# One decoder layer with 32 experts: all expert pairs in written order, side work split over four places

## The chip, the cores and the metric

The kernel runs on one core of one Trainium2 chip. The metric is the device time of one execution in microseconds. Three runs of the kernel before took 611.28, 612.3 and 613.26 us; the median, 612.3, is what the prediction is measured against. One further execution was profiled.

## The reference, cut to what matters

All data are float32; 256 tokens of 1024 features, one layer.

```python
h = x
a = rms_norm(h, g_mix);  z = a @ w_in                  # pool channels | q | k | v | forget logits
h = h + concat(causal_pool_mixer(...), forgetting_attention(...)) @ w_out
# hierarchical mixture of experts: 4 groups of 8 experts, each 1024 -> 512 -> 1024
t = rms_norm(h, g_ffn)
grp = argmax(t @ w_grp + b_grp)                        # one group per token
top2 of the 8 experts of that group, weights comb      # two experts per token
for g in range(4):
    hg = einsum('nd,edf->nef', t, w_e_gate[g]);  hu = einsum('nd,edf->nef', t, w_e_up[g])
    y += einsum('nef,efd->nd', silu(hg) * hu * comb[:, g, :, None], w_e_down[g])
h = h + y
gate = sigmoid(rms_norm(h, g_ple) @ w_ple_gate)        # 1024 x 1024
h = h + gate * (p @ w_ple_proj)
out = rms_norm(h, g_final)
```

The weights of the 32 experts are 201 MB of the 221 MB that are read.

## The kernel before, in words

The first part (mixer, attention, output projection, routing) is not touched by the change. Then come the experts in 16 **pairs** of two, `pi` 0 to 15. Each expert has 32 slots for tokens; four experts (two pairs) make a **quad** `q`, eight experts (four pairs) a **group** `g` of up to 128 tokens.

For a pair, `gate_up(pi, kh)` (L927) multiplies the slots' rows by the gate and up weights, half of the 1024 inputs at a time (`kh`). Two experts times gate and up are four 32-column tiles, written to four quarters of one accumulator, so that four matmuls with different column tiles stand side by side on TensorE. A float32 matmul counts as two in the profile. `hidden` (L938) is SiLU on ScalarE and a product on VectorE; `hidden_transposes` (L944) four transposes and a copy; `down` (L953) the down weights, again with four column tiles; `stack` (L965) copies the result to `ys`, one half on ScalarE, one on VectorE.

Beside the pairs stands work by group and quad, with full-width matmuls:
- `compact(g)` (L869) collects a group's rows `Xc` with matmuls; `one_hots`, `gather(q, kh)` (L902) and `scatter_weights(q)` (L913) make a quad's inputs `xgs` and the matrix `sws`; `scatter(q)` (L972) adds the experts' results by token in accumulators `Y`.
- When a group's two quads are done: `add_rows` (L1062) adds `Y` to the rows on VectorE, `half_norm` (L1068) makes the norm (squares on ScalarE, eight small steps on VectorE), `turn` (L1082) transposes the rows, `z_direct(g, ms)` (L1091) multiplies them by the gate matrix in eight steps `m` (the accumulators `Z`), `embedding_rows` (L1102) picks the group's rows of the embedding, and `finish` (L1113) applies the gate, the last norm and writes the rows with an indirect DMA of GpSimd.

`group_ends` and `group_body` (L1283 to L1313) put this work in lists `todo[pi][0..2]`, which `fill` calls at three places of a pair: after the first half of gate-up, after `hidden`, and after `stack`. The last group can't wait for its last quad: before pair 15, `last_slots`, `turn`, and `z_direct` of group 3 run on the rows as they are, and what the quad's results add to Z is added later (`z_rows` for pair 14, `z_rows1` for pair 15, whose two experts 30 and 31 are worked one after the other).

What sets the order: up to L1042 and from L1358 on, TensorE, VectorE and ScalarE run in the order in which the code is written (`manual_schedule`). Between, for pairs 2 to 14, a planner decides, by its own costs and due times, in which order each engine runs what the code asks for; the calls of `fill` only set priorities there. At pair 8 stands a conditional block (`dense_path`, not taken with these inputs).

The weights come in pieces of 1 MiB through SyncE's queue into buffers of that size that are used in turn (`stream`, L789); a piece is issued when the matmuls that read the buffer's last content are done. Twelve pieces make a pair: gate and up of both experts for the first input half, the same for the second, then down. PSUM has two buffers for accumulators of a pair (`acc`), two for transposes and gathers (`tb_`) and four for `Y` and `Z`.

Of the kernel before, what the change touches and what calls it, by code (L numbers as in the profile page):

```python
# [13 lines left out]
AF = mybir.ActivationFunctionType  # L14
# [10 lines left out]
def layer_kernel(ctx, tc, x, p, g_mix, w_in, b_f, w_pool, s_pool, w_out, g_ffn, w_grp, b_grp,  # L25
                 w_rt, b_rt, w_e_gate, w_e_up, w_e_down, g_ple, w_ple_gate, w_ple_proj, g_final, out):
    nc = tc.nc
# [3 lines left out]
    NP, NQ = NE // 2, NE // 4  # L31
# [8 lines left out]
    def acc(name):  # L40
        return psA.tile([128, 512], F32, tag="acc", name=name)

    def tb_(name):
        return psA.tile([128, 512], F32, tag="t", name=name)
# [113 lines left out]
    def sumsq(dst, src, name):  # L158

        junk = wk.tile([128, src.shape[1]], BF, tag="b", bufs=2, name=name)  # L160
        return nc.scalar.activation(junk, src, AF.Square, scale=D ** -0.5, accum_out=dst)
# [84 lines left out]
    for g, w in enumerate(WINDOWS):  # L246
# [2 lines left out]


    in_order = ExitStack()
    in_order.enter_context(tc.manual_schedule(engines={mybir.EngineType.PE, mybir.EngineType.DVE,
                                                       mybir.EngineType.Activation}))
    aTh = region(0, "aTh", F32R).rearrange("p (k t) -> p k t", k=8)
    aTl = region(1, "aTl", F32R).rearrange("p (k t) -> p k t", k=8)

# [600 lines left out]
    def small(g):  # L857
        if g not in smalls:
            smalls[g] = st.tile([128, 8], F32, name=f"small{g}")
        return smalls[g]  # L860

    def in_group(g):

        pg_ = wk.tile([128, 2, 128], F32, tag="c0", name=f"ing{g}")
        for tb in range(2):
            nc.vector.tensor_scalar(pg_[:, tb, :], place1, place[:, tb, g:g + 1], None, op0=ALU.is_equal)
        return pg_
# [76 lines left out]
    def hidden_transposes(pi, act):  # L944
        pa = tb_(f"pa{pi}")
        for c in range(4):
            nc.tensor.transpose(pa[:, c * 64:(c + 1) * 64], act[64:128, c * 128:(c + 1) * 128],  # L947
                                ident[64:128, 64:128])
        at = wk.tile([128, 4, 64], F32, tag="b", bufs=2, name=f"at{pi}")
        nc.vector.tensor_copy(at, pa[:, :256].rearrange("p (c s) -> p c s", c=4))  # L950
        return at

    def down(pi, act, dn):  # L953

        at = hidden_transposes(pi, act)
        pd = acc(f"pd{pi}")
        for c in range(4):
            for gI in range(4):
                j, dh = gI % 2, gI // 2
                nc.tensor.matmul(pd[32 * gI:32 * gI + 32, :], lhsT=at[:, c, 32 * j:32 * j + 32],  # L960
                                 rhs=dn[j, c // 2](c % 2)[:, dh * 512:(dh + 1) * 512],
                                 start=c == 0, stop=c == 3, tile_position=(0, 32 * gI))
        return pd
# [75 lines left out]
    for kh in range(2):  # L1039
        gather(1, kh, orr)  # L1040
    scatter_weights(1, oq)
    in_order.close()  # L1042


    gpm = gp.rearrange("p q k -> p (q k)")
    hTs, PPc, Z, ss3, r3 = {}, {}, {}, {}, {}
    LG = 3

    def chunk2(m):
# [12 lines left out]
    def add_rows(g):  # L1062

        for dh in range(2):
            xs = Xc[g][:, dh * 512:(dh + 1) * 512]
            nc.vector.tensor_add(xs, xs, Ys[g][dh])

    def half_norm(g):  # L1068

        s = small(g)[:, 1:3]  # L1070
        for dh in range(2):
            sumsq(s[:, dh:dh + 1], Xc[g][:, dh * 512:(dh + 1) * 512], f"sq3{g}{dh}")
        r3[g] = small(g)[:, 3:4]
        rsqrt(r3[g], s[:, 0:1], s[:, 1:2], f"r3s{g}", 0.5)

# [23 lines left out]
                nc.tensor.matmul(Z[g][i][:, 0:c], lhsT=hTs[g][:, m, :], rhs=wpg[m // 2](m % 2)[:, c * i:c * i + c],  # L1099
                                 start=m == 0, stop=m == 7 and g != LG)  # L1100

    def embedding_rows(g):  # L1102

        pg_ = in_group(g)
        PPc[g] = fins[g][:, 1024:2048]
        for dh in range(2):
            ds = slice(dh * 512, (dh + 1) * 512)
            pp = tb_(f"ppc{g}{dh}")
            for tb in range(2):
                nc.tensor.matmul(pp, lhsT=pg_[:, tb, :], rhs=PP[:, tb, ds], start=tb == 0, stop=tb == 1)  # L1110
            nc.scalar.activation(PPc[g][:, ds], pp, AF.Copy, scale=0.5)

    def finish(g, sg, o):  # L1113

# [100 lines left out]
        nc.gpsimd.dma_start(out[0].rearrange("(b p) d -> p b d", p=128), X)  # L1215


    def rows_of_quad(q, khs=range(2)):
        if 0 in khs:
            oqs[q] = one_hots(q)  # L1220
        for kh in khs:
            gather(q, kh, oqs[q][1])
        if 1 in khs:
            scatter_weights(q, oqs[q][0])

    oqs = {}
    yTs, zls, ysl, zsl = {}, {}, {}, {}
# [49 lines left out]
    def new_fin(g):  # L1277
        fins[g] = fin_tile(g)

    def scatter_q(q):  # L1280
        scatter(q, yss[q])

    def group_ends(g):  # L1283

        p, e = 4 * g, g - 1
        todo[p][0] += [lambda: scatter_q(2 * g - 1), lambda: add_rows(e), lambda: half_norm(e)]
        todo[p][1] += [lambda: rows_of_quad(2 * g + 1, (0,))]
        todo[p][2] += [lambda: rows_of_quad(2 * g + 1, (1,)), lambda: new_fin(e), lambda: turn(e, 0),
                       lambda: turn(e, 1)]
        ends = [lambda: embedding_rows(e), lambda: finish(e, fins[e][:, 0:1024], fins[e][:, 1024:2048])]  # L1290
        if g == LG:
            todo[p][2] += [lambda: z_direct(e, range(0, 3))]
            todo[p + 1][0] += [lambda: z_direct(e, range(3, 6))]
            todo[p + 1][1] += [lambda: z_direct(e, range(6, 8)), ends[0]]
            todo[p + 1][2] += [ends[1]]
        else:
            todo[p + 1][0] += [lambda: z_direct(e, range(0, 3))]
            todo[p + 1][1] += [lambda: z_direct(e, range(3, 5))]
            todo[p + 1][2] += [lambda: z_direct(e, range(5, 7))]
            todo[p + 2][0] += [lambda: z_direct(e, range(7, 8))]  # L1300
            todo[p + 2][1] += [ends[0]]
            todo[p + 2][2] += [ends[1]]

    todo = {pi: [[], [], []] for pi in range(2, NP - 1)}

    def group_body(g):
        todo[4 * g + 2][0].append(lambda: scatter_q(2 * g))
        todo[4 * g + 2][1].append(lambda: row_numbers(g))
        if g < LG:
            todo[4 * g + 3][0].append(lambda: compact(g + 1))  # L1310
            todo[4 * g + 3][1].append(lambda: rows_of_quad(2 * g + 2, (0,)))
            todo[4 * g + 3][2].append(lambda: rows_of_quad(2 * g + 2, (1,)))

    for g in range(4):
        group_body(g)
        if g:
            group_ends(g)
    todo[2][2].append(lambda: embedding(*emb))
    todo[4][1].append(last_gain)
    todo[12][0] += [lambda: new_fin(LG), lambda: embedding_rows(LG)]  # L1320
    todo[14][0] += [lambda: add_rows(LG)]
    todo[14][1] += [last_slots, lambda: turn(LG, 0), lambda: turn(LG, 1), lambda: z_direct(LG, range(0, 2))]
    todo[14][2] += [lambda: gained(14), lambda: z_direct(LG, range(2, 8))]
    rv = nc.values_load(ovi[0:1, 0:1], min_val=0, max_val=1)

    def fill(pi, n):
        for f in todo[pi][n]:
            f()

    for pi in range(2, NP - 1):  # L1330
        gu, dn = pair_w
        if pi == 2:
            PP = region(whole_region(), "PP").rearrange("p (b d) -> p b d", b=2)
            emb = load_embedding()
        if pi == 4:
            wpg = load_gate()
            r_ht = whole_region()
            gfB = quarter(3, "gfB")
        if pi == 8:
            fill(pi, 0)  # L1340
            with tc.If(rv > 0):  # L1341
                dense_path()
        pair_w = load_pair(pi + 1)
        pg = acc(f"pg{pi}")
        gate_up(pi, 0, gu, pg)
        if pi != 8:
            fill(pi, 0)
        if pi % 2 == 0:
            yss[pi // 2] = quarter(1, f"ys{pi // 2}")
        gate_up(pi, 1, gu, pg)  # L1350
        act = hidden(pi, pg)
        fill(pi, 1)
        pd = down(pi, act, dn)
        stack(pi, pd, yss[pi // 2])
        fill(pi, 2)


    ctx.enter_context(tc.manual_schedule(engines={mybir.EngineType.PE, mybir.EngineType.DVE,  # L1358
                                                  mybir.EngineType.Activation}))
    pi, Q = NP - 1, NQ - 1  # L1360
    gu, dn = pair_w
    ys, Zl = yss[Q], Z[LG]
# [87 lines left out]
                                 rhs=wpg[m // 2](m % 2)[:, 256 * g:256 * g + 256],  # L1450
                                 start=m == 0, stop=m == 7, tile_position=(0, 32 * g))

    z_rows(pi - 1, range(2))
    gate_up1(0, 0)
    z_rows(pi - 1, range(2, 6))
    gate_up1(0, 1)
    hidden1(0)
    z_rows(pi - 1, range(6, 8))
    hidden_transposes1(0)
    for dh in range(2):  # L1460
        down1(0, dh, lambda c: dn[0, c // 2](c % 2)[:, 512 * dh:512 * dh + 512])
    for dh in range(2):
        gained1(0, dh)
        for g in range(4):
            nc.gpsimd.tensor_copy(ys[rows_of(0), chunk2(4 * dh + g)], wide[32 * g:32 * g + 32, 0, dh, :])
# [25 lines left out]
    ys1 = y_last(1)  # L1491
    z_rows1(1, range(4, 8))
    add_last(1, ys1)
    half_norm(LG)
    pair_of((zh, zlo), zl1[1][:, 0:256])

    for g in range(4):
        rs = slice(32 * g, 32 * g + 32)
        for n, part in enumerate((zh, zlo)):
            nc.tensor.matmul(Zl[g][:, 0:256], lhsT=sw1[rs, :], rhs=part[rs, :], start=False, stop=n == 1,  # L1500
                             tile_position=(32 * g, 0))
    finish(LG, fins[LG][:, 0:1024], last_o)


# [26 lines left out]
```

## Time and profile before

| what | value |
|---|---|
| median of three runs | 612.3 us (611.28 to 613.26) |
| the profiled execution | 611.7 us, its span 610.1 us |
| TensorE matmul busy | 534.2 us (88%) |
| VectorE, ScalarE, GpSimd busy | 176.4, 117.9, 40.7 us |
| moved by DMA | 222.54 MB, 365 GB/s over the span |
| TensorE's granted clock, mean | 0.937 |

The span runs from the first to the last instruction; the execution takes 1.6 us more. "Busy" of TensorE is from the start of matmuls to their modelled ends, so matmuls on several column tiles count once. A clock of 1.0 is 2.4 GHz, 0.5 is 1.2 GHz; a stretch's value is the mean over it. The chain of waits goes back from the last instruction, at each step to what released it or to the instruction before it on its engine.

### The profile page before, as it was taken

The numbers are of one execution on the slowest core, as the hardware profiler recorded it, in microseconds if no ns is written. First come the engines' busy times: TensorE is split into PE (matmuls) and PEld (weight loads), VectorE is DVE, ScalarE is ACT, GpSimd is POOL, SyncE is SP. The second block draws the span as 40 slices with busy tenths as digits, with TensorE's granted clock in tenths as the row PEclk, the third lists the DMA queues.
The fourth block names the chain that finished last, engine by engine and source line by source line (L and its number), as shares of the span: only waits on it lengthen the run. The fifth ranks groups of instructions, "written<-read, shape, count | busy, mean of one in ns | idle before, by whom it ended". The sixth has DMA issues, their size and how long they took to land. (4 is left out here: it accounts for less than half of the span.)

```text
span 610.1 us, 7828 instructions
## 1 busy us (share of the span) xinstructions
PE 534.2 (88%) x3139; PEld 253.8 (42%) x3139; DVE 176.4 (29%) x461; ACT 117.9 (19%) x246; POOL 40.7 (7%) x82
## 2 busy tenths in 40 slices
PE   7999999978899999987976799989797998997890
PEld 6899778533333434221312233223141332452450
DVE  5677665233111221030303110223022103301234
ACT  4553564111011110110201000111011002000142
POOL 6095000000000000000000000000000000000100
PEclk9999999699989889997879789999799899999996
DMA  8989957599999999999999999999999999999400
GB/s 293 342 291 417 404 203 274 232 414 415 408 418 415 416 417 421 413 420 413 421 414 419 411 417 413 414 414 416 414 413 415 414 414 416 413 371 367 172 2 17
DMA packets 55734, 222.54 MB, mean 365 GB/s; under 512 B 8714, under 2 KB 15630, under 8 KB 42254
## 3 DMA queue, kind: packets, MB, share of 16 engines
q1 hardware_dynamic: 55086, 220.94, 90.9%
q0 software_dynamic: 608, 1.05, 0.5%
q8 instruction: 26, 0.43, 0.3%
q14 instruction: 14, 0.11, 0.1%
HBM read 220.93 MB, written 2.10 MB: 366 GB/s over the span
## 5 line engine op out<-in xcount | busy, mean ns | idle before, releaser
L934 PE MATMUL pg<-wu,xg 128*32 128x512 f32 x480 | 131.0, 641 | 11.6 <-DMA wu<-in_w_e_up_dram 11.6
L934 PE MATMUL pg<-wg,xg 128*32 128x512 f32 x472 | 132.8, 639 | 9.3 <-PEq L1341 5.8
L960 PE MATMUL pd<-wd,at 128*32 128x512 f32 x480 | 80.8, 668 | 3.3 <-DVE at L950 1.6
L1099 PE MATMUL Z<-wpg,fin 128*128 128x512 f32 (+1 forms) x160 | 60.9, 521 | 0.9 <-DVE fin L1087 0.9
L941 DVE TENSOR_TENSOR act<-act,pg 64x512 f32<-64x512 f32 x15 | 10.4, 692 | 174.4 <-ACT act L940 174.4
L934 PEld LDWEIGHTS pg<-wu,xg 128*32 128x32 f32 x480 | 29.8, 116 | 65.8 <-issue 39.9
L934 PEld LDWEIGHTS pg<-wg,xg 128*32 128x32 f32 x472 | 28.8, 115 | 56.5 <-issue 44.9
L1099 PEld LDWEIGHTS Z<-wpg,fin 128*128 128x128 f32 x160 | 28.6, 189 | 34.1 <-issue 31.2
L940 ACT ACTIVATE act<-pg 64x512 f32<-64x512 f32 x15 | 8.8, 589 | 167.6 <-PE pg L934 167.6
L908 PEld LDWEIGHTS pgx<-oq,xrows 128*128 128x128 f32 x112 | 28.2, 331 | 15.2 <-issue 10.4
L960 PEld LDWEIGHTS pd<-wd,at 128*32 128x32 f32 x480 | 16.0, 118 | 43.8 <-issue 36.1
L908 PE MATMUL pgx<-oq,xrows 128*128 128x128 f32 x112 | 32.2, 425 | 1.3 <-ACT xrows L883 1.3
L1130 POOL DMA_INDIRECT out_dram<-fin,rowi x3 | 3.0, 1005 | 400.1 <-DVE fin L1129 400.1
L947 PE MATMUL pa<-ident,act 64*128 64x64 f32 x60 | 6.9, 235 | 18.7 <-DVE act L941 18.7
L910 DVE TENSOR_TENSOR xg<-pgx,gf 128x512 f32<-128x512 f32 x14 | 9.7, 692 | 42.6 <-PE pgx L908 42.6
L968 DVE COPY ys<-pd 64x512 f32<-64x512 f32 x15 | 10.4, 694 | 39.7 <-ACT ys L967 39.7
L967 ACT COPY ys<-pd 64x512 f32<-64x512 f32 x15 | 8.7, 578 | 62.5 <-PE pd L960 62.4
L275 PE MATMUL po<-sp_o,cTh 128*128 128x512 f32 x64 | 20.7, 404 | 0.0
L978 PE MATMUL Y<-ys,sw 128*128 128x512 f32 x28 | 15.8, 687 | 3.6 <-ACT ys L967 3.6
L947 PEld LDWEIGHTS pa<-ident,act 64*128 64x128 f32 x60 | 4.8, 138 | 32.2 <-DVE act L941 30.5
L1110 PE MATMUL ppc<-PP,ing 128*128 128x512 f32 x32 | 16.3, 622 | 0.0
L882 PE MATMUL xc<-X,ing 128*128 128x512 f32 x32 | 15.8, 617 | 0.0
(360 smaller groups left out, 678.2 us busy)
## 6 DMA issues: line engine op xcount, KB each, us to landing
wu<-in_w_e_up_dram SPq DMA_DIRECT2D x52, 1024.0 KB, 12.6
wg<-in_w_e_gate_dram SPq DMA_DIRECT2D x49, 1024.0 KB, 13.4
wd<-in_w_e_down_dram SPq DMA_DIRECT2D x49, 1024.0 KB, 19.1
wd<-in_w_e_down_dram SPq DMA_DIRECT2D x30, 512.0 KB, 10.9
wg<-in_w_e_gate_dram SPq DMA_DIRECT2D x28, 512.0 KB
wu<-in_w_e_up_dram SPq DMA_DIRECT2D x24, 512.0 KB, 15.4
w_o<-in_w_out_dram SPq DMA_DIRECT2D x4, 1024.0 KB, 5.8
wpg<-in_w_ple_gate_dram SPq DMA_DIRECT2D x4, 1024.0 KB, 16.3
```

The lines of the kernel that those rows point to most:

```text
L275: nc.tensor.matmul(o, lhsT=a, rhs=b, start=first and i == 0, stop=last and i == 2)
L882: nc.tensor.matmul(px, lhsT=pg_[:, tb, :], rhs=X[:, tb, ds], start=tb == 0, stop=tb == 1)
L908: nc.tensor.matmul(pg[:, k4 * 128:(k4 + 1) * 128], lhsT=Xc[q // 2][:, 4 * kh + k4::8], rhs=orr, start=True, stop=True)
L910: nc.vector.tensor_tensor(xgs[q][:, 4 * kh:4 * kh + 4, :], pg.rearrange("p (k t) -> p k t", k=4), gf[:, 4 * kh:4 * kh + 4, None].to_broadc ...
L934: nc.tensor.matmul(pg[32 * c:32 * c + 32, :], lhsT=xg[:, k, sl:sl + 32], rhs=gu["gu"[c // 2], j, kh](k % 4), start=k == 0, stop=k == 7, ti ...
L941: nc.vector.tensor_mul(act[64:128, :], act[64:128, :], pg[64:128, :])
L947: nc.tensor.transpose(pa[:, c * 64:(c + 1) * 64], act[64:128, c * 128:(c + 1) * 128], ident[64:128, 64:128])
L960: nc.tensor.matmul(pd[32 * gI:32 * gI + 32, :], lhsT=at[:, c, 32 * j:32 * j + 32], rhs=dn[j, c // 2](c % 2)[:, dh * 512:(dh + 1) * 512], s ...
L968: nc.vector.tensor_copy(ys[rs, 512:1024], pd[64:128, :])
L978: nc.tensor.matmul(Ys[g][dh], lhsT=sws[q], rhs=ys[:, dh * 512:(dh + 1) * 512], start=q % 2 == 0, stop=q % 2 == 1 or last)
L1099: nc.tensor.matmul(Z[g][i][:, 0:c], lhsT=hTs[g][:, m, :], rhs=wpg[m // 2](m % 2)[:, c * i:c * i + c], start=m == 0, stop=m == 7 and g != LG)
L1110: nc.tensor.matmul(pp, lhsT=pg_[:, tb, :], rhs=PP[:, tb, ds], start=tb == 0, stop=tb == 1)
```

## The change

Pairs 2 to 14 now run in written order on TensorE, VectorE and ScalarE as well; only the conditional block at pair 8 is left to the planner. The lists have four places: after the first half of gate-up (0), after `hidden` (1), between the transposes' copy and the down matmuls (2, new), and after `stack` (3). The work is dealt out anew: Z in single steps, the two halves of `embedding_rows` separately, `add_rows` and `half_norm` later, and the norm cut into squares and root. Embedding rows of group 3 stand at pair 11 instead of 12; at pair 14 group 3's rows, `last_slots`, `turn` and the first Z step stand in place 0, and Z steps 6 and 7 go into pair 15, where `z_rows` of pair 14 move back behind gate-up and down of expert 30. At the very end the root of the norm stands behind the split of the last Z rows.

```diff
-    in_order.enter_context(tc.manual_schedule(engines={mybir.EngineType.PE, mybir.EngineType.DVE,
-                                                       mybir.EngineType.Activation}))
+    ordered = {mybir.EngineType.PE, mybir.EngineType.DVE, mybir.EngineType.Activation}
+    in_order.enter_context(tc.manual_schedule(engines=ordered))
...
         at = hidden_transposes(pi, act)
+        if between:
+            between()
         pd = acc(f"pd{pi}")
...
     scatter_weights(1, oq)
-    in_order.close()
...
+    def plan(pi, *places):
+        for have, new in zip(todo[pi], places):
+            have.extend(new)
+
+    def zs_of(g, *ms):
+        return [lambda m=m: z_direct(g, (m,)) for m in ms]
+
+    def quad_rows(q):
+
+        return ([lambda: new_quad(q), lambda: gather(q, 0, oqs[q][1])], [lambda: gather(q, 1, oqs[q][1])],
+                [lambda: scatter_weights(q, oqs[q][0])])
+
+    def group_body(g):
+        plan(4 * g + 2, [lambda: scatter_q(2 * g), lambda: row_numbers(g)])
+        if g < LG:
+            plan(4 * g + 3, [lambda: compact(g + 1)], *quad_rows(2 * g + 2))
+
     def group_ends(g):
 
         p, e = 4 * g, g - 1
...
+        rows = quad_rows(2 * g + 1)
+        plan(p, [lambda: scatter_q(2 * g - 1)], rows[0], rows[1] + [lambda: add_rows(e)],
+             rows[2] + [lambda: new_fin(e), lambda: turn(e, 0), lambda: turn(e, 1), lambda: half_norm(e)])
+        emb2 = [lambda dh=dh: embedding_rows(e, dh) for dh in range(2)]
+        end = [lambda: finish(e, fins[e][:, 0:1024], fins[e][:, 1024:2048])]
         if g == LG:
...
+            plan(p, [], [], [], zs_of(e, 0, 1))
+            plan(p + 1, zs_of(e, 2, 3, 4), zs_of(e, 5), zs_of(e, 6), zs_of(e, 7) + emb2 + end)
         else:
...
+            plan(p + 1, zs_of(e, 0, 1, 2), zs_of(e, 3), zs_of(e, 4), zs_of(e, 5, 6, 7))
+            plan(p + 2, [], emb2[:1], emb2[1:], end)
...
+    plan(2, [], [], [], [lambda: embedding(*emb)])
+    plan(4, [], [], [], [last_gain])
+    plan(11, [], [], [], [lambda: new_fin(LG), lambda: embedding_rows(LG, 0), lambda: embedding_rows(LG, 1),
+                          lambda: row_numbers(LG)])
+    plan(14, [lambda: add_rows(LG), last_slots, lambda: turn(LG, 0), lambda: turn(LG, 1)] + zs_of(LG, 0),
+         zs_of(LG, 1, 2), zs_of(LG, 3), zs_of(LG, 4, 5) + [lambda: gained(14)])
...
-        pd = down(pi, act, dn)
+        pd = down(pi, act, dn, lambda: fill(pi, 2))
         stack(pi, pd, yss[pi // 2])
-        fill(pi, 2)
-
-
-    ctx.enter_context(tc.manual_schedule(engines={mybir.EngineType.PE, mybir.EngineType.DVE,
-                                                  mybir.EngineType.Activation}))
+        fill(pi, 3)
...
-    z_rows(pi - 1, range(2))
     gate_up1(0, 0)
-    z_rows(pi - 1, range(2, 6))
+    z_direct(LG, (6, 7))
     gate_up1(0, 1)
     hidden1(0)
-    z_rows(pi - 1, range(6, 8))
+    z_rows(pi - 1, range(2))
     hidden_transposes1(0)
+    z_rows(pi - 1, range(2, 3))
     for dh in range(2):
         down1(0, dh, lambda c: dn[0, c // 2](c % 2)[:, 512 * dh:512 * dh + 512])
+    z_rows(pi - 1, range(3, 8))
...
-    half_norm(LG)
+    half_squares(LG)
     pair_of((zh, zlo), zl1[1][:, 0:256])
+    half_root(LG)
```

## Rows read from the trace of the kernel before

**Rows 1.** Page, 40 slices of 15.25 us: TensorE, its clock, DMA in tenths, GB/s.
```profile
PE   7999999978899999987976799989797998997890
PEclk9999999699989889997879789999799899999996
DMA  8989957599999999999999999999999999999400
GB/s 293 342 291 417 404 203 274 232 414 415 408 418 415 416 417 421 413 420 413 421 414 419 411 417 413 414 414 416 414 413 415 414 414 416 413 371 367 172 2 17
```

**Rows 2.** Windows: stretch, length, busy time (instructions) by engine, TensorE's clock, DMA share, GB/s.
```profile
280.00:345.00 65.00, 51.20 (x241) 16.90 (x245) 12.91 (x39) 7.38 (x16) 1.08 (x1) 0.82 1.02 415
345.00:468.00 123.00, 108.68 (x520) 35.80 (x512) 22.93 (x57) 13.76 (x27) 0.96 (x1) 0.96 1.02 414
530.00:560.00 30.00, 27.35 (x155) 13.76 (x153) 1.20 (x3) 1.17 (x2) 0.00 (x0) 1.00 0.93 366
571.00:610.00 39.00, 23.14 (x364) 13.31 (x356) 16.02 (x46) 13.92 (x37) 3.58 (x9) 0.85 0.03 10
471.74:584.84 113.10, 103.70 (x673) 44.40 (x673) 20.74 (x43) 13.73 (x30) 3.56 (x9) 0.97 0.87 350
```

**Rows 3.** Chain of waits from 468 to 590 us: start, length, engine, tile, line, instructions.
```profile
468.08 3.63 PE pg L934 x26
...
481.61 1.12 PE Z L1099 x2
...
491.11 0.97 PE pg L934 x2
...
494.00 0.97 PE pg L934 x2
494.97 3.63 PE Z L1099 x8
498.60 0.98 PE pg L934 x2
...
501.49 3.56 PE pg L934 x28
...
514.34 0.60 ACT act L940
...
522.07 0.59 ACT ys L967
...
573.89 1.14 issue
...
583.11 1.73 PE pg L1380 x32
```

**Rows 4.** Timeline of SyncE's queue, 522 to 560 us: start, length, the loads issued.
```profile
523.90 3.01 SPq L799 DMA_DIRECT2D wg<-in_w_e_gate_dram  x1
539.37 0.34 SPq L799 DMA_DIRECT2D wu<-in_w_e_up_dram  x1
...
557.96 1.67 SPq L799 DMA_DIRECT2D wd<-in_w_e_down_dram  x2
```

**Rows 5.** Timeline of TensorE where it waits for the last up-weights (pairs 11, 12).
```profile
436.78 1.06 PE L934 MATMUL pg<-wu,xg 128*32 128x512 f32 x1 [0.97 <-DMA wu<-in_w_e_up_dram]
...
468.08 0.62 PE L934 MATMUL pg<-wu,xg 128*32 128x512 f32 x1 [1.48 <-DMA wu<-in_w_e_up_dram]
```

**Rows 6.** Timeline of TensorE at the gather of a quad's first half.
```profile
454.48 1.93 PE L908 MATMUL pgx<-oq,xrows 128*128 128x128 f32 x8
```

**Rows 7.** VectorE groups from 400 us on: line, shapes, count, busy us, mean ns, idle before.
```profile
L1122 DVE SCALAR_TENSOR_TENSOR fin<-fin 128x512 f32<-128x512 f32 x4 | 2.8, 688 | 20.1 <-ACT fin L1111 18.7 <-ACT fin L1120 1.3
...
L896 DVE TENSOR_TENSOR oq<-auxc,slot 128x128 f32<-128x128 f32 x2 | 0.6, 288 | 0.0
```

**Rows 8.** Timeline from 594 to 598 us: first step of the root, split of Z.
```profile
595.02 0.21 DVE L133 TENSOR_SCALAR r3s<-small 128x1 f32<-128x1 f32 x1 [0.80 <-ACT sq L161]
...
596.62 0.41 DVE L1412 TENSOR_TENSOR zhl<-zl,zhl 128x256 fp32r<-128x256 f32 x1
```

More of the change, by code (lines that the diff above doesn't have):

```diff
@@ L951, in hidden_transposes, with down @@
         return at
-    def down(pi, act, dn):
+    def down(pi, act, dn, between=None):
         at = hidden_transposes(pi, act)
+        if between:
+            between()
         pd = acc(f"pd{pi}")
@@ L1041, in layer_kernel @@
     scatter_weights(1, oq)
-    in_order.close()
     gpm = gp.rearrange("p q k -> p (q k)")
-    hTs, PPc, Z, ss3, r3 = {}, {}, {}, {}, {}
+    hTs, PPc, Z, r3, ings = {}, {}, {}, {}, {}
     LG = 3
@@ L1068, in half_norm, with half_squares, half_root @@
     def half_norm(g):
+        half_squares(g)
+        half_root(g)
+    def half_squares(g, dhs=range(2)):
+        for dh in dhs:
+            sumsq(small(g)[:, 1 + dh:2 + dh], Xc[g][:, dh * 512:(dh + 1) * 512], f"sq3{g}{dh}")
+    def half_root(g):
         s = small(g)[:, 1:3]
-        for dh in range(2):
-            sumsq(s[:, dh:dh + 1], Xc[g][:, dh * 512:(dh + 1) * 512], f"sq3{g}{dh}")
         r3[g] = small(g)[:, 3:4]
@@ L1100, in z_direct, with embedding_rows @@
                                  start=m == 0, stop=m == 7 and g != LG)
[L1102 to L1111, printed above, removed]
+    def embedding_rows(g, dh):
+        if dh == 0:
+            ings[g] = in_group(g)
+            PPc[g] = fins[g][:, 1024:2048]
+        ds = slice(dh * 512, (dh + 1) * 512)
+        pp = tb_(f"ppc{g}{dh}")
+        for tb in range(2):
+            nc.tensor.matmul(pp, lhsT=ings[g][:, tb, :], rhs=PP[:, tb, ds], start=tb == 0, stop=tb == 1)
+        nc.scalar.activation(PPc[g][:, ds], pp, AF.Copy, scale=0.5)
     def finish(g, sg, o):
@@ L1215, in dense_path, with new_quad @@
         nc.gpsimd.dma_start(out[0].rearrange("(b p) d -> p b d", p=128), X)
[L1218 to L1224, printed above, removed]
+    def new_quad(q):
+        oqs[q] = one_hots(q)
     oqs = {}
@@ L1281, in scatter_q @@
         scatter(q, yss[q])
+    todo = {pi: [[], [], [], []] for pi in range(2, NP - 1)}
+    def plan(pi, *places):
[10 more added lines that the diff above has]
+            plan(4 * g + 3, [lambda: compact(g + 1)], *quad_rows(2 * g + 2))
@@ L1283, in group_ends @@
     def group_ends(g):
         p, e = 4 * g, g - 1
[L1286 to L1290, printed above, removed]
+        rows = quad_rows(2 * g + 1)
@@ L1291, in group_ends @@
+        plan(p, [lambda: scatter_q(2 * g - 1)], rows[0], rows[1] + [lambda: add_rows(e)],
+             rows[2] + [lambda: new_fin(e), lambda: turn(e, 0), lambda: turn(e, 1), lambda: half_norm(e)])
+        emb2 = [lambda dh=dh: embedding_rows(e, dh) for dh in range(2)]
+        end = [lambda: finish(e, fins[e][:, 0:1024], fins[e][:, 1024:2048])]
         if g == LG:
-            todo[p][2] += [lambda: z_direct(e, range(0, 3))]
-            todo[p + 1][0] += [lambda: z_direct(e, range(3, 6))]
-            todo[p + 1][1] += [lambda: z_direct(e, range(6, 8)), ends[0]]
@@ L1295, in group_ends @@
-            todo[p + 1][2] += [ends[1]]
-        else:
[L1297 to L1312, printed above, removed]
+            plan(p, [], [], [], zs_of(e, 0, 1))
@@ L1317, in layer_kernel @@
             group_ends(g)
[L1318 to L1323, printed above, removed]
+    plan(2, [], [], [], [lambda: embedding(*emb)])
[4 more added lines that the diff above has]
+         zs_of(LG, 1, 2), zs_of(LG, 3), zs_of(LG, 4, 5) + [lambda: gained(14)])
     rv = nc.values_load(ovi[0:1, 0:1], min_val=0, max_val=1)
@@ L1340, in layer_kernel @@
             fill(pi, 0)
+            in_order.close()
             with tc.If(rv > 0):
                 dense_path()
+            in_order.enter_context(tc.manual_schedule(engines=ordered))
         pair_w = load_pair(pi + 1)
@@ L1502, in layer_kernel @@
     finish(LG, fins[LG][:, 0:1024], last_o)
+    in_order.close()
 _INS = ['x', 'p', 'g_mix', 'w_in', 'b_f', 'w_pool', 's_pool', 'w_out', 'g_ffn', 'w_grp', 'b_grp',
```

## The prediction

> **What bounds the kernel now.** I read the slices of the page first [rows 1]. From about 122 us to 530 us the DMA engines are full and move 411 to 421 GB/s, so the weight stream sets the pace there; TensorE is busy 70 to 99% beside it. Then the rate sags (371, 367, 172 GB/s in slices 36 to 38), and after it there is no traffic. The windows give sizes [rows 2]: 414 to 415 GB/s from 280 to 468 us, 366 from 530 to 560, and 39 us after the last weights (571 to 610) in which almost nothing is loaded.
>
> Next the chain of waits from 468 us on [rows 3]. Its first row there is TensorE starting on the last up-weights of pair 12, which landed at 468.08; from that point no link of the chain is a transfer. TensorE is behind the stream: pair 13's gate-up begins in single pieces at 491.11, and the last gate-up piece of pair 15 starts at 583.11 and ends at 584.84. The SyncE timeline says the same from the other side [rows 4]: after a load issued by 526.91 it issues nothing until 539.37, since the buffers are not released, and the last two loads start at 557.96. So: the stream bounds until 468, TensorE from 468 to 585, and a chain through ScalarE and VectorE from 585 to the end. Only the last two can move by an order of work.
>
> **Part 1: work that is no longer cut up.** In the chain, two matmuls of one 32-column tile stand alone between full-width ones: 0.97, 0.97 and 0.98 us at 491.11, 494.00 and 498.60, and the other 28 of that half then take 3.56 us as if all 32 were there [rows 3]. The tile alone takes almost as long as four tiles side by side. Such a lone pair costs 0.95 us; the chain has 11 of them between 475 and 546 us (one in pair 12's down part before the Z work and one after it, three in pair 13's first half, one in its second, three and two in pair 14's halves). In written order each half of gate-up and each down part is one block. 11 x 0.95 = 10.5 us go.
>
> The Trainium skill ("TensorEngine Tiling (Array Packing)", Key Properties) says that a change of tiling mode drains TensorE. By that rule alone the loss would be the drain at each switch; the row nearest to it is a Z group of two at 1.12 us (481.61) against 0.91 for two of a run of eight (494.97, 3.63 us) [rows 3], so 0.1 to 0.2 us, some 2 us in all, and the change would be worth 2 us here. The rows above decide against it: they show a whole pass lost, not a drain.
>
> **Part 2: work between 471.74 (pair 12's SiLU) and 584.84.** TensorE is busy 103.70 of these 113.10 us [rows 2]; 9.4 are waits. Minus the 10.5 above; minus 3.4 for the two stretches of half clock (mean 0.97 over the window: 3% of 113 us, which at half clock is 6.8 us, 1.2 GHz instead of 2.4, of which half is lost); plus 1.93 for the gather of quad 7's first half, which stood at 454.48 [rows 6] and now comes behind pair 12's SiLU. That leaves 91.7 us of work at full clock. The half-clock time I count as gone because its return would mostly lie in the waits on transfers below.
>
> **Part 3: the waits that the written order makes.** Going through the queue in order, with durations from the rows: SiLU 0.60 and ScalarE's copy 0.59 [rows 3], a pass of VectorE over 512 columns 0.69, a one-hot 0.29 [rows 7]:
> - Pair 12: the gather sits behind two one-hots that sit on VectorE behind the product and so behind SiLU, 0.60+0.69+0.58: 1.9. The down part, behind the two gathers and their products: 0.6. The scatter-weight transpose waits for the one-hot product, queued on VectorE behind both halves of the copy of the down result: 0.59+0.69+0.29 and the signals between, 1.7. Pair 12 is done at 489.2.
> - Pair 13: half of gate-up 3.5, three Z steps 5.6, so the second half could start at 498.2. The last up-weights of pairs 11 and 12 landed 31.3 us apart (436.78, 468.08) [rows 5]; at 31.2 per pair the next land at 499.3: 1.1. Z then lies over SiLU, product and copy, which costs nothing (without Z it would be the 1.4 us of before). The second half of the down weights, 10.4 us (4/12 of a pair) later, at 509.7: 1.0. Last Z and embedding products end at 517.1.
> - Pair 14: its first half is there at 520.1: 3.0. After it and the two scatters (525.4) the transposes wait for VectorE: the finish of group 2 starts when the embedding copies are off (tanh at 517.8), and takes four passes of 0.69 [rows 7], the norm's eight small steps (1.68, 595.02 to 596.70) [rows 8] and one pass, to 524.5; row numbers, two additions (0.69) and one-hots follow to 527.0: 1.7. The second half starts at 530.9, its weights landed at 530.5. From here on TensorE is behind the stream. Down ends at 543.9, the last transposes of pair 14 at 549.0.
> - Pair 15: the second down part waits for the first one's copy (0.4, two accumulators in turn), the Z rows of expert 30 for a gain behind the copy of Z rows 14 (1.1). The 1.14 us stall of before at 573.89, where the transposed hidden copy was queued behind that copy [rows 3], goes.
>
> Sum of waits, with 0.2 of crumbs: 12.7, so more than the 9.4 of before; the SiLU waits of pairs 13 and 14 (1.4 each) go, waits on weights come. 471.74 + 91.7 + 12.7 = 576.1 for the end of the last gate-up piece, 8.7 earlier than 584.84.
>
> **Part 4: stream and tail.** With gate-up 13 and 14 consumed 12 to 20 us earlier than before, SyncE's long gap [rows 4] closes and the rate of 530 to 560 us returns to 414: (414-366)x30/414 = 3.5 us, so the last weights land at 567 to 570, some 6 us ahead of their use near 577. The tail is the same except that VectorE now makes the low part of the last Z rows (0.41 at 596.62) before the root instead of behind it. The root starts 0.4 later and the tanh needs it: the root would be ready 1.68 after 596.2, at 597.9 in the old time, against a tanh at 597.5: +0.4 [rows 8]. Bounds: nothing, if the last product is late anyway, to 1.3 (a whole root behind it).
>
> **Part 5: edits counted at nothing.** Embedding rows of group 3 move from pair 12 to 11, add_rows and half-norm to later places, row numbers of group 3 are made twice (0.35 us). All before 468 us lies beside the stream: the fullest pair there, 5 or 9, has 26 us of TensorE work by the same durations against 31.2. If that cover were gone, each of them costs its own time. No DMA is added; loads keep their order.
>
> Sum: 610.1 - 8.7 + 0.4 = 601.8 of span; the profiled execution took 611.7, 1.6 over its span, and lies 0.6 below the median 612.3. On the median: 612.3 - 8.3 = 604.0.
>
> **Rivals.**
> (a) *Half clock, slower.* TensorE's clock falls to 1.2 GHz after it has idled: between 280 and 345 us, paced by the stream, the mean is 0.82 [rows 2], so 36% of the time at half. Pairs 13 and 14 become paced by the stream. If 471 to 574 ran like that, 0.36 x 102 = 37 us at half lose 18.4 us of work; the waits on weights and VectorE, about 7, take part of it, 11.5 remain: 615.5. It decides from 8.3+7 = 15.3 us lost, 31 us at half clock. Against it: the same stretch had only 6.8 us of that before with 9.4 of waits, and behind 531 no wait of over 1.1 us is left. A mild form, three to five us lost at places without cover, gives 607 to 609. The Trainium skill ("TensorE: Matmul & The Clock Gate", Why this matters for your kernels) asks for no idle gaps between bursts of matmuls because the clock then falls back; the 0.82 agrees with it.
> (b) *The stream sets the end.* If the tail behind the last weights stays 39 us, whatever is in it, only the 3.5 us of lost rate return: 612.3 - 3.5 = 608.8. For it: transfers are full for two thirds of the span. Against it: before, 14 us of gate-up and Z rows stood between the last landing and the last piece; that is backlog, not latency.
> (c) *No change.* The written order might do again what the old order did, or new waits of 20 us instead of 12.7 (a VectorE or ScalarE queue that I read wrongly) eat the gain: 610.5 to 614. Against: the cut-up order can't come from text in blocks.
>
> **Chances.** Forecast (600 to 606.5, or a little better) 0.62; (a) mild 0.13; (b) 0.10; (c) 0.08; (a) full 0.07. A difference under 0.3% (1.8 us) can't be told from none here. Faster by over 0.3%: 0.62+0.13+0.10 = 0.85; same 0.08; slower 0.07. The low end takes the landings at the rate of 414 GB/s by bytes (2.5 us earlier, worth 1.6) and a free tail edit and 2 us of waits less; the high end takes in (b) and mild (a): 599 to 610.5.
>
> **What would show it.** Right: gate-up and down blocks of 3.5 us without lone pieces from 471 on; pair 13's second half starting on a landing near 499, pair 14's near 530; the last gate-up piece ending near 576; 410 GB/s to 565 us. Wrong: mean clock under 0.9 in 471 to 574; TensorE waits of over 3 us on VectorE or ScalarE; a tail of over 27 us behind the last gate-up piece; a first difference of over 1 us before 468.

## The result, and the profile after

The changed kernel took 604.43 us (median; 603.68 to 605.81), the kernel before 612.38 us on the same chip (611.28 to 613.26): a ratio of 0.9874, 95% interval 0.9849 to 0.9898, or 7.95 us less. 604.0 had been forecast. The profiled execution of the changed kernel is the longest of its four: 605.81 us, span 604.2, which is 2.4 us over the 601.8 of the sum. So the total is right and the parts are worth a closer look.

The page first, its 40 slices (15.1 us each): TensorE, its clock, GB/s. They answer to [rows 1]: slices 36 and 37 now move 416 and 412 GB/s where 371 and 367 stood, and the last weights come in slice 38.

```profile
PE   8999999988878888997778588977787789799890
PEclk9989999899989787999997779999879799989995
GB/s 290 346 285 417 384 226 257 235 412 415 407 418 415 418 414 420 415 418 416 417 417 418 412 413 417 411 417 411 418 413 416 417 411 415 412 416 412 242 2 17
```

The windows of the changed kernel (columns as in [rows 2]). TensorE's busy time between 345 and 468 us fell from 108.68 to 102.11 us with no effect on the end of that stretch, which is the stream's. From 530 to 560 it is 415 GB/s in place of 366. The last two windows are for the account below.

```profile
345.00:468.00 123.00, 102.11 (x528) 36.59 (x520) 22.82 (x59) 13.32 (x27) 0.97 (x1) 0.93 1.02 414
530.00:560.00 30.00, 30.00 (x212) 18.46 (x212) 3.74 (x6) 1.54 (x3) 0.00 (x0) 0.93 1.02 415
571.00:604.20 33.20, 18.05 (x280) 10.55 (x280) 14.28 (x44) 11.41 (x32) 0.98 (x1) 0.82 0.03 9
528.20:534.30 6.10, 6.10 (x23) 4.67 (x27) 1.38 (x2) 0.33 (x2) 0.00 (x0) 0.52 1.02 412
474.38:578.58 104.20, 94.90 (x681) 46.71 (x681) 24.95 (x61) 14.49 (x34) 3.31 (x9) 0.95 0.92 371
```

The chain of waits of the changed kernel, to be held against [rows 3]: the blocks are whole (3.57 us for 32 matmuls of a half), no lone pair is left, and the last gate-up piece ends at 576.85 + 1.73 = 578.58 (584.84 before). The first block, behind the landing at 469.02 (468.08 before), takes 5.33 us for the 26 matmuls that took 3.63.

```profile
469.02 5.33 PE pg L934 x26
...
492.86 3.57 PE pg L934 x32
496.43 5.35 PE Z L1106 x12
501.77 3.57 PE pg L934 x32
...
534.30 3.57 PE pg L934 x32
...
576.85 1.73 PE pg L1387 x32
```

TensorE's waits from 465 to 600 us (what waits, what it waits for, us in all, how often, longest). The only waits on weights are those of pair 12, the last of them at 469.02.

```profile
PE sw1p L1273 <- DVE oq L1270: 3.1, 1, 3.1
PE pgx L908 <- DVE oq L899: 2.1, 1, 2.1
PE pg L934 <- DMA wu<-in_w_e_up_dram: 2.0, 2, 1.5
PE sw7p L920 <- DVE oc L917: 1.8, 1, 1.8
PE zl L1456 <- DVE yT L1447: 1.4, 1, 1.4
PE pd L1409 <- ACT last L1413: 0.4, 1, 0.4
...
PE pgx L908 <- DVE xg L910: 0.4, 1, 0.4
```

The timeline, rows that answer to [rows 4] and [rows 8]. SyncE has no gap of 12 us any more; its last two loads are issued at 554.89 (557.96 before). At the end the split of Z stands before the root, whose first step starts at 589.86; the tanh follows the root at 591.62.

```profile
536.16 2.72 SPq L796 DMA_DIRECT2D wd<-in_w_e_down_dram  x2
541.02 2.87 SPq L796 DMA_DIRECT2D wg<-in_w_e_gate_dram  x2
546.00 2.88 SPq L796 DMA_DIRECT2D wu<-in_w_e_up_dram  x2
...
554.89 1.65 SPq L799 DMA_DIRECT2D wd<-in_w_e_down_dram  x2
...
589.52 0.42 DVE L1419 TENSOR_TENSOR zhl<-zl,zhl 128x256 fp32r<-128x256 f32 x1 [1.56 <-ACT zhl L1418]
589.86 0.20 DVE L133 TENSOR_SCALAR r3s<-small 128x1 f32<-128x1 f32 x1
...
591.62 0.84 ACT L1127 ACTIVATE fin<-Z,small 128x256 f32<-128x256 f32 x2 [2.14 <-DVE small L147]
```

### The profile page after: what moved, and what is told of

Its sections match the earlier page's. It is cut to its first block, busy times and chain, and to the rows that moved or that the text cites. A ratio compares the mean times of both kernels' runs of the same rounds, so it can differ in the third digit from the quotient of the medians.

```text
span 604.2 us, 7842 instructions
## 1 busy us (share of the span) xinstructions
PE 511.1 (85%) x3139; PEld 256.5 (42%) x3139; DVE 175.1 (29%) x463; ACT 116.5 (19%) x246; POOL 39.9 (7%) x82
## 3 DMA queue, kind: packets, MB, share of 16 engines
q0 software_dynamic: 608, 1.05, 0.5%
## 4 chain that ended last, share of the span: by engine, by line
DMA 48%; PE 42%; DVE 4%; ACT 2%; issue 2%; SPq 0%; POOLq 0%; ACTq 0%; DVEq 0%
DMA wu<-in_w_e_up_dram 20%; DMA wd<-in_w_e_down_dram 14%; DMA wg<-in_w_e_gate_dram 11%; PE pg L934 7%; PE Z L1106 5%; PE pd L962 4%; PE po L275 4%; DMA wpg<-in_w_ple_gate_dram 2%; PE ps_u L275 2%; PE ps_k L275 2%; PE ps_q L275 2%; PE pgx L908 1%; PE g L661 1%; PE zl L1456 1%; PE zl L1250 1%
## 5 line engine op out<-in xcount | busy, mean ns | idle before, releaser
L934 PE MATMUL pg<-wg,xg 128*32 128x512 f32 x472 | 123.9, 640 | 5.6 <-PEq L1349 4.5
L962 PE MATMUL pd<-wd,at 128*32 128x512 f32 x480 | 66.1, 687 | 2.7 <-issue 1.5
L934 PEld LDWEIGHTS pg<-wg,xg 128*32 128x32 f32 x472 | 27.0, 115 | 56.9 <-issue 50.8
L908 PE MATMUL pgx<-oq,xrows 128*128 128x128 f32 x112 | 30.8, 439 | 15.3 <-DVE oq L899 13.1
L1106 PEld LDWEIGHTS Z<-wpg,fin 128*128 128x128 f32 x160 | 30.0, 197 | 29.1 <-issue 26.4
L980 PE MATMUL Y<-ys,sw 128*128 128x512 f32 x28 | 13.8, 615 | 0.0
L275 PE MATMUL ps_u<-aTh,sp_u 128*128 128x256 f32 x64 | 13.5, 307 | 0.0
L275 PE MATMUL ps_k<-aTh,sp_k 128*128 128x256 f32 x64 | 12.6, 290 | 0.0
## 6 DMA issues: line engine op xcount, KB each, us to landing
wg<-in_w_e_gate_dram SPq DMA_DIRECT2D x28, 512.0 KB, 15.1
```

The costliest lines, as they stand in the source:

```text
L275: nc.tensor.matmul(o, lhsT=a, rhs=b, start=first and i == 0, stop=last and i == 2)
L908: nc.tensor.matmul(pg[:, k4 * 128:(k4 + 1) * 128], lhsT=Xc[q // 2][:, 4 * kh + k4::8], rhs=orr, start=True, stop=True)
L934: nc.tensor.matmul(pg[32 * c:32 * c + 32, :], lhsT=xg[:, k, sl:sl + 32], rhs=gu["gu"[c // 2], j, kh](k % 4), start=k == 0, stop=k == 7, ti ...
L980: nc.tensor.matmul(Ys[g][dh], lhsT=sws[q], rhs=ys[:, dh * 512:(dh + 1) * 512], start=q % 2 == 0, stop=q % 2 == 1 or last)
```

## The experiments

### Which part of the change carries it

**Order without lists**: the kernel before, with pairs 2 to 14 in written order.

```diff
     scatter_weights(1, oq)
-    in_order.close()
...
         if pi == 8:
             fill(pi, 0)
+            in_order.close()
             with tc.If(rv > 0):
                 dense_path()
+            in_order.enter_context(tc.manual_schedule(engines=ordered))
```

> The kernel before with its own lists and three places, only that pairs 2 to 14 run in written order. Theory T (the gain is the blocks: no lone column-tile pieces behind 468 us): no lone pieces, 10.5 us of TensorE work gone, waits of 10 to 13 us as in the changed kernel but at other places; 604 to 607 us. Rival L (the new dealing over four places brings the gain): 610 us or slower, as SiLU and the copies stand bare.

Measured: 609.62 us, ratio to before 0.9957 (0.9937 to 0.9977), between the two expectations. Its chain shows why. TensorE runs whole blocks and stands on the stream at pair 14's second half, whose landing it waits for. But from 528.19 to the end of the last gate-up piece (581.36) it needs 53.2 us, where the changed kernel needs 44.3 from the start of the same half (534.30 to 578.58): the old lists put the turning of group 3's rows and all its Z steps behind that landing (16 and 48 matmuls). That makes 5.1 of the 8.9 us (TensorE busy 47.62 us against 42.48); the other 3.8 are waits (5.55 against 1.80), the longest of them 2.4 us for VectorE behind pair 14's SiLU, which stands bare there, as the rival had it.

```profile
528.19 3.63 PE pg L934 x26
...
535.96 5.41 PE Z L1098 x16
...
548.11 10.56 PE Z L1098 x48
...
581.36 1.06 PE Z L1431 x4
```

**Lists without order**: the changed kernel with the planner back for pairs 2 to 14.

```diff
     scatter_weights(1, oq)
+    in_order.close()
...
-            in_order.close()
             with tc.If(rv > 0):
                 dense_path()
-            in_order.enter_context(tc.manual_schedule(engines=ordered))
...
+    in_order.enter_context(tc.manual_schedule(engines=ordered))
     pi, Q = NP - 1, NQ - 1
```

> The changed kernel's lists and four places, but the planner orders pairs 2 to 14 as before. Theory T: the planner cuts blocks into lone pieces again, about ten behind 468 us, time 609 to 614 us. Rival L: 603 to 606 us.

Measured: 613.96 us, ratio 1.0042 (1.0009 to 1.0074): a little slower than before. Ten lone pairs are back in its chain, some of them here:

```profile
493.40 0.98 PE pg L934 x2
494.38 1.91 PE Z L1107 x4
496.29 0.98 PE pg L934 x2
...
500.90 0.98 PE pg L934 x2
501.87 1.91 PE Z L1107 x4
503.79 3.56 PE pg L934 x28
```

So neither half of the change is worth the whole: order alone -2.3 us, lists alone +2.0, both -7.95. The order takes out the lone pairs; the lists see to it that what TensorE then does ahead of the last landings is what would otherwise stand behind them.

**Late pairs alone, early pairs alone**: written order from pair 12 on, or only up to pair 11, with the new lists in both.

```diff
     scatter_weights(1, oq)
+    in_order.close()
...
-            in_order.close()
             with tc.If(rv > 0):
                 dense_path()
+        if pi == 12:
             in_order.enter_context(tc.manual_schedule(engines=ordered))
```

```diff
             in_order.enter_context(tc.manual_schedule(engines=ordered))
+        if pi == 12:
+            in_order.close()
...
+    in_order.enter_context(tc.manual_schedule(engines=ordered))
     pi, Q = NP - 1, NQ - 1
```

> The changed kernel with written order only from pair 12 on; pairs 2 to 11 are left to the planner. Theory T (before 468 us all lies beside the stream): 604.4 as the changed kernel, within 1.5. Rival E (the early pairs have a part in the gain): 606 to 611.

> Written order for pairs 2 to 11 alone, the planner for pairs 12 to 14, new lists throughout. Theory T, the early pairs lie beside the weight stream and have no part: the time is that of the new lists with the planner everywhere, 614 us (612.5 to 615.5), with lone pieces of 0.97 us behind 468 us. Rival E, the early order brings a part of the gain: 608 to 611 us.

Measured: late alone 604.62 us (603.11 to 607.01), ratio 0.9887 (0.9841 to 0.9932); early alone 613.13 us, ratio 1.0039 (1.0011 to 1.0066), with ten lone pairs in its chain behind 468 us again. Within what these runs can tell (the four executions of late alone lie 3.9 us apart), the late pairs are the whole gain; the early ones lie beside the stream, as part 5 had it.

### What a lone pair costs

In the changed kernel, the six matmul pairs of Z steps 2 to 4 are put between single column tiles of pair 13's first half; nothing is added.

```diff
                                  tile_position=(0, 32 * c))
+                if cuts and c < 3:
+                    cuts.pop(0)()
...
-            plan(p + 1, zs_of(e, 2, 3, 4), zs_of(e, 5), zs_of(e, 6), zs_of(e, 7) + emb2 + end)
+            plan(p + 1, [], zs_of(e, 5), zs_of(e, 6), zs_of(e, 7) + emb2 + end)
...
-        gate_up(pi, 0, gu, pg)
+        gate_up(pi, 0, gu, pg, [lambda m=m, d=d: z_direct(2, (m,), (d,)) for m in (2, 3, 4) for d in range(2)]
+                if pi == 13 else [])
```

> The changed kernel, but in pair 13's first half of gate-up six Z matmuls of 512 columns (steps 2, 3, 4) are put between single column tiles; no work added or left out. Theory T (a lone tile costs a whole pass): that half and its Z take 4.5 to 5.7 us longer than 8.9, and the end moves by 4 to 6 us, to 608.5 to 610.5. Rival D (only a drain of 0.1 to 0.2 us at each of the twelve switches): 1.2 to 2.4 us longer, 605.5 to 607. Rival S (the stream sets the end): 604.4, nothing moves.

Measured: 609.57 us, 5.1 over the changed kernel, ratio to before 0.9952 (0.9933 to 0.9971). The chain:

```profile
490.66 0.98 PE pg L934 x2
491.64 1.05 PE Z L1108 x2
492.69 0.97 PE pg L934 x2
...
502.86 6.12 PE pg L934 x50
508.98 1.06 PE Z L1108 x2
```

Both halves of gate-up 13 and the three Z steps take 490.66 to 508.98, 18.32 us; whole, in the changed kernel's chain above, 3.57 + 5.35 + 3.57 = 12.49. So 5.83 us for six cuts, 0.97 for each. Of these, 4.85 us lie in the column tiles, whose pieces in the chain add up to 11.99 us in place of 7.14, and 0.98 in the six Z pairs, which take 1.05 to 1.06 us each in place of 0.89. The drain of the Trainium skill ("TensorEngine Tiling (Array Packing)", Key Properties), at the 0.1 to 0.2 us that the prediction read for it, would be 1.2 to 2.4 us here for the twelve switches; this run decides against it as the measure of the loss, though the 0.16 us on each Z pair are of its size.

### What is left: VectorE's queue at pairs 12 and 14

**Finish split.** The 3.1 us wait is for the scatter weights of pair 14, queued on VectorE behind the finish of group 2. `finish` is cut in two: the tanh (`gate_of`) stays where it is; VectorE's part and the output (`rest_of`) go to the end of pair 14.

```diff
-            plan(p + 1, zs_of(e, 2, 3, 4), zs_of(e, 5), zs_of(e, 6), zs_of(e, 7) + emb2 + end)
+            plan(p + 1, zs_of(e, 2, 3, 4), zs_of(e, 5), zs_of(e, 6), zs_of(e, 7) + emb2 + [lambda: gate_of(e, fins[e][:, 0:1024])])
...
-         zs_of(LG, 1, 2), zs_of(LG, 3), zs_of(LG, 4, 5) + [lambda: gained(14)])
+         zs_of(LG, 1, 2), zs_of(LG, 3), zs_of(LG, 4, 5) + [
+             lambda: gained(14), lambda: rest_of(2, fins[2][:, 0:1024], fins[2][:, 1024:2048])])
```

> The changed kernel, but of group 2's finish only the two tanh stay at pair 13's end; its VectorE passes and the norm go behind the last transposes of pair 14. Theory T (behind 468 us TensorE's queue is the bound, with the waits of pair 14 in it): the 3.1 us wait for VectorE shrinks to about 1.6, the half clock behind it shortens or goes, pair 14's second half starts 1.5 to 4.5 us earlier and the end with it: 600 to 603 us. Rival S (stream or tail set the end): 604.4.

Measured: 608.42 us, ratio 0.9951 (0.9929 to 0.9974): a miss, and slower than the changed kernel. The wait did shrink to 1.4 us, but another took its place: pair 15's down part waits 4.7 us for ScalarE's copy of its predecessor.

```profile
PE pd L1416 <- ACT last L1420: 4.7, 1, 4.7
...
PE sw1p L1279 <- DVE oq L1276: 1.4, 1, 1.4
```

The chain says what that copy waited for: the indirect DMA that writes group 2's rows reads its source until 563.74, 8.37 us from its issue, and `last`, the tile that ScalarE's copy writes, lies in the same buffer (`region(r_ht, ...)`).

```profile
555.37 8.37 DMA out_dram<-fin,rowi
...
563.84 0.28 ACT last L1420
564.12 0.04 issue
564.17 1.93 PE pd L1416 x32
```

**Split, output sooner.** The same split with `rest_of` in place 2 of pair 14, between Z step 3 and the down part.

```diff
-         zs_of(LG, 1, 2), zs_of(LG, 3), zs_of(LG, 4, 5) + [
-             lambda: gained(14), lambda: rest_of(2, fins[2][:, 0:1024], fins[2][:, 1024:2048])])
+         zs_of(LG, 1, 2), zs_of(LG, 3) + [lambda: rest_of(2, fins[2][:, 0:1024], fins[2][:, 1024:2048])],
+         zs_of(LG, 4, 5) + [lambda: gained(14)])
```

> Finish of group 2 split again, its VectorE and output part now in place 2 of pair 14, so that the output transfer (8.4 us in the split before) is issued some 7 us sooner. Theory H, the 4.7 us wait of pair 15's first down part was the transfer still reading the buffer: that wait is under 0.5 us, the wait for pair 14's scatter weights stays at about 1.4 us (3.1 in the changed kernel), and the time is 601.5 to 603.5 us. Rival V, the split itself is what costs (VectorE's five passes are late for something else wherever they stand): 606 us or more.

Measured: 601.26 us (600.82 to 601.53), ratio 0.9830 (0.9799 to 0.9861), a little under the 601.5 to 603.5 expected and the lowest median of all kernels run here. Each of its four executions lies below the changed kernel's lowest, 603.68, but the intervals of the two ratios (0.9849 to 0.9898 there) overlap, so that the size of this step is less sure than the end of the wait. In its timeline the output DMA is issued at 544.48, and TensorE's wait for the copy is 0.4 us again:

```profile
544.48 0.96 POOL L1143 DMA_INDIRECT out_dram<-fin,rowi  x1 [116.12 <-ACT ys L969]
```

```profile
PE sw1p L1279 <- DVE oq L1276: 1.4, 1, 1.4
...
PE pd L1416 <- ACT last L1420: 0.4, 1, 0.4
```

The buffer's wait was the cause of the miss, not the split.

**Quad 7 sooner; both; the tail undone.** One-hots of quad 7 ahead of pair 12's `hidden`, its scatter weights in place 2; then that with the first split; and the changed kernel with the root ahead of the split of Z, as before.

```diff
+        if g == LG:
+            plan(p, [lambda: new_quad(q), lambda: scatter_q(q - 2)], [lambda: gather(q, 0, oqs[q][1])],
+                 [lambda: gather(q, 1, oqs[q][1]), lambda: scatter_weights(q, oqs[q][0]), lambda: add_rows(e)], tail)
+        else:
...
-    half_squares(LG)
+    half_norm(LG)
     pair_of((zh, zlo), zl1[1][:, 0:256])
-    half_root(LG)
```

> The changed kernel, but in pair 12 the one-hots of quad 7 stand ahead of hidden and the scatter weights beside the second gather. Theory T: the waits of 2.1 and 1.8 us there go; part of it is eaten by the wait for pair 13's and 14's weights and by VectorE in pair 14; 601 to 604 us. Rival S: 604.4.

> Both edits. Theory T: pair 14's second half of gate-up is then reached near the landing of its weights (528 us in the runs with written order so far) instead of 534.3; 5 to 6 us less, 598.5 to 600.5 us, and no less, since the stream bounds there. Rival S: 604.4. If half clock follows waits, its share behind 468 us falls below 5 us (13.7 us in the changed kernel).

> The changed kernel with the last root ahead of the split of the last Z rows again, as before. By the prediction's step the tail behind the last gate-up piece gets 0.4 us shorter (25.2 instead of 25.6 in the profile); if that root is not on the chain, nothing. The time itself can't show it.

Measured: quad 7 sooner 602.45 us, ratio 0.9858 (0.9809 to 0.9908); with the first split 607.59, ratio 0.9935 (0.9916 to 0.9954), where 598.5 to 600.5 had been expected: a miss, with the same buffer's wait (4.8 us). The half clock did not fall as expected either: from 468 us to the end of the last gate-up piece the mean clock is 0.94, as in the changed kernel. The tail undone, one execution: 602.13 us, and from the end of the last gate-up piece (575.23) to the end of the span (600.5) 25.3 us, against 25.6 in the changed kernel: the 0.4 of part 4 within 0.1. The two kernels below that have this edit show 25.3 and 25.2 us, and two without it (quad 7 sooner, the split with its output sooner) 25.6 each, so the step is clear in the traces, though the time can't show it.

**Do the gains add?** All three (split in place 2), and quad 7 with the tail.

> Three edits together on the changed kernel: finish split as in the run beside it, quad 7's one-hots and scatter weights earlier, the root ahead of the split of the last Z rows. If the gains add (about 1.5, 2.0 and 0.35 us from 604.4): 599.5 to 601.5 us, last gate-up piece ending at 573 to 575 us. Rival, the half clock takes back what the waits give: 602 to 604 us.

> Quad 7's one-hots and scatter weights earlier, and the root ahead of the split of the last Z rows; finish as in the changed kernel. If they add: 602.45 less 0.35 = 602.1 us (601.3 to 602.9), tail behind the last gate-up piece 25.3 us. Rival, the tail edit hides behind another wait: 602.5 to 603.5 us, tail 25.6.

Measured: all three 602.56 us (600.19 to 603.98), ratio 0.9838 (0.9802 to 0.9875), so not the 599.5 to 601.5 of gains that add; quad 7 with the tail 602.55 (600.30 to 603.94), ratio 0.9849 (0.9808 to 0.9890), within the 601.3 to 602.9 expected if those two add. The intervals of these kernels and of the single edits overlap, so that the times alone do not decide. The half clock, named as a rival for all three, is not what holds them up at pair 14: both have a clock of 1.00 from 528 to 540 us. The timelines of TensorE tell more. In all three of these kernels it waits for the last up-weights of pair 14's first half, first the split in place 2, then all three, then quad 7 with the tail:

```profile
518.82 0.62 PE L934 MATMUL pg<-wu,xg 128*32 128x512 f32 x1 [1.01 <-DMA wu<-in_w_e_up_dram]
```

```profile
522.14 0.62 PE L934 MATMUL pg<-wu,xg 128*32 128x512 f32 x1 [1.44 <-DMA wu<-in_w_e_up_dram]
```

```profile
520.23 0.62 PE L934 MATMUL pg<-wu,xg 128*32 128x512 f32 x1 [1.48 <-DMA wu<-in_w_e_up_dram]
```

From that landing to the end of the span it is 80.6, 80.3 and 80.3 us. What is saved ahead of it, as at quad 7, is waited out there; the tail's 0.3 us show. Behind the landing the split and quad 7 shorten the same wait: the one for pair 14's scatter weights, 3.1 us in the changed kernel (2.4 with the tail undone), is 1.4 with the split, 1.5 with quad 7 and the tail, and 1.4 with all three, so the second of the two edits finds little left. And where the landing falls (518.8 to 522.1 in these profiled executions) sets the rest. Up to pair 12 the first two of these kernels do the same, so that spread is the execution's and not the edit's. Most of it is older than the full stream: the wait for pair 10's up-weights ends at 405.74 in the first and 408.48 in the second, and a load of the first part, which no edit touches, is issued 2.5 us apart, again the split in place 2 first, then all three:

```profile
56.78 0.38 SPq L799 DMA_DIRECT2D wd<-in_w_e_down_dram  x1
```

```profile
59.30 0.38 SPq L799 DMA_DIRECT2D wd<-in_w_e_down_dram  x1
```

What makes the first part longer in one execution was not settled.

## Why the prediction was right, step by step

The end of the last gate-up piece was forecast at 576.1 and came at 578.58. Between SiLU of pair 12 and that end, 104.4 us were forecast (471.74 to 576.1) and 104.20 measured: the sum held, its terms did not.

- **Part 1, lone pieces: right.** None is left behind 468 us, and 0.97 us for each is what they cost when put back; 0.95 had been taken.
- **Part 2, work: wrong by the half clock.** "The half-clock time I count as gone" was the step that failed. TensorE was busy 94.90 us from SiLU on, not 91.7, at a mean clock of 0.95; and the block ahead of SiLU took 5.33 us in place of 3.63, so that SiLU came at 474.38 (0.9 us from the landing, 1.7 from this block). The largest single place is 528.20 to 534.30, straight behind the 3.1 us wait for VectorE: clock 0.52, 1.2 GHz for nearly all of it, 6.1 us of work where 3.9 had been forecast. Half clock came behind shorter waits too: 0.52 from 480 to 483 us, after the 2.1 us wait for VectorE that ended at 476.46. The Trainium skill ("TensorE: Matmul & The Clock Gate", Why this matters for your kernels) warns that the clock falls back behind idle gaps; here it did. In the three kernels above where the same wait is 1.4 to 1.5 us, 528 to 540 us ran at 1.00 (0.75 in the changed kernel), but another with 1.5 us (quad 7 sooner) had 0.86, so the wait alone does not settle it.
- **Part 3, waits: the total 3.4 us too high, in two terms.** 12.7 had been forecast, 9.3 came (104.20 less 94.90). The 5.1 us on weights of pairs 13 and 14 did not come in this execution: TensorE, 2.6 us late at SiLU, ended pair 13 at 518.6 (517.1 forecast) and found the weights there. With the same order of work a little more punctual (late pairs alone, tail undone) pair 14 waited 0.46 us until 519.28 and 0.63 until 518.18, where 3.0 until 520.1 had been forecast. So most of the term was too large in itself, and not only hidden: no kernel with the new lists and written order waits for the weights of pair 13; in the eight profiles that show the landing at pair 14 it comes 50.5 to 51.2 us behind pair 12's, not 52.0; and TensorE works six matmuls of that half, 1.1 us, before it needs the last piece. The longest wait there was 1.5 us. VectorE's 1.7 at pair 14 were 3.1, the finish of group 2 starting later than forecast behind that same delay. The rest was read well: 1.9, 0.6, 1.7, 0.4 and 1.1 forecast, 2.1, 0.4, 1.8, 0.4 and 1.4 measured.
- **Part 4, stream and tail: right.** 415 GB/s from 530 to 560, the last loads issued 3.1 us earlier (3.5 from the rate), the tail 25.6 us (25.3 before, 25.7 forecast).
- **Part 5, early edits: right**, by the run of the late pairs alone.
- **The signs.** Whole blocks of 3.57 us, a mean clock of 0.94 from 471 to 574 us and a tail of 25.6 us came as for a right forecast. Two did not: a wait of 3.1 us on VectorE came, which had been named as a sign of being wrong, and neither second half (501.77 and 534.30) started on a landing.
- **Readings of the rows.** Three were slightly off, and no term rests on them: in [rows 1] slice 11 moved 408 GB/s (411 to 421 was said) and TensorE's digit in slice 22 is 6 (70 to 99% was said); in [rows 3] two of the "other 28" matmuls at 501.49 belong to the next half.

So +2.6 us at the start, +3.2 of work and -3.4 of waits make the 2.4 us by which this span missed; the other three executions were 1 to 2 us shorter, and the median came out 0.4 us from the forecast. That is partly luck: the half clock and the missing waits on weights are two errors of opposite sign. Only a small part of them is linked, since a TensorE that works more slowly meets its weights landed: as an estimate from the 50.5 us above, the landing at pair 14 fell near 519.5 here, and a TensorE on time would have waited about 1.3 us for it, not 5.1. Of the rivals, (a) came in its mild size, about ten microseconds at half clock (0.95 over 104.20 us), which cost five at most, but the total hid it; (b) was wrong for this change, yet a landing, that of pair 14's first half, is what now bounds the three kernels that improve on it.

## What to carry to other kernels

Look in the chain for single column tiles between full-width matmuls: each cut cost 0.97 us here, about a whole pass, and an order that keeps blocks whole gets it back, provided that the work put between them is placed so that little stands behind the last landing. When a forecast removes waits behind a stream, find the first landing that TensorE will again wait for: what is saved ahead of it is not saved. Two edits that shorten the same wait do not add. Before moving an output to a later place, see what else uses its source buffer.

## What the runs showed of the hardware that was not expected

- The indirect DMA that writes a group's rows held its source for 8.37 us after its issue, while the DMA engines ran at full rate (412 GB/s from 555 to 564 us in that run).
- Two profiled executions with the same loads in the same order had the same piece landed 3.3 us apart (518.82 and 522.14), of which 2.7 us were there at 405 us and 2.5 at 59 us, where the kernels do not differ yet. That is more than most single edits here are worth.
